# Softmax blocks transposed by DMA instead of TensorE in a two-layer decoder kernel

## Chip, cores and metric

The kernel runs on one core of a Trainium2 chip. The metric is the device time of one execution in microseconds (us).

## The reference, cut

One RG-LRU layer, then one layer of multi-head latent attention over shared keys and values. What matters here is the attention (1024 positions, 8 heads, blocks of 128 queries, all fp32):

```python
def one_block(args):                      # 128 queries of every head
    qn_b, qr_b, bi = args
    s = jnp.einsum("bqhd,bkhd->bhqk", qn_b, k_nope) + jnp.einsum("bqhr,bkr->bhqk", qr_b, k_rope)
    s = s * ATTN_SCALE
    mask = kpos[None, :] <= (bi * Q_BLOCK + jnp.arange(Q_BLOCK))[:, None]
    s = jnp.where(mask[None, None], s, -jnp.inf)
    p = jax.nn.softmax(s, axis=-1)
    return jnp.einsum("bhqk,bkhd->bqhd", p, v)
...
y = o.reshape(bsz, seq, N_HEADS * V_DIM) * jax.nn.silu(gate)
return y @ w_out                          # + residual, then a last rms_norm
```

## The kernel before

All products run on TensorE in a rounded fp32 format (`F32R`), three matmuls for one product: every operand is split by `hl` into a rounded part `hi` (on ACT) and a rest `lo` (on DVE), and hi*hi + hi*lo + lo*hi are summed in PSUM. The RG-LRU layer and the projections come first (about 530 us); their results wait in DRAM (`x1d`, `kvd`, `qsd`, the gates `gd`). SBUF holds most of its tiles in `NPAGES` = 36 pages of 128x1024 words.

The attention is a loop over 64 items (head `hd`, query block `qb`). In the order of the program:

- `scores` (lines 846 to 870): five matmuls per up to 512 keys into a PSUM tile `s` (two buffers, of two banks each), then on DVE the causal mask and the negative maximum, on ACT the exponential with its sum, on DVE the reciprocal and the scaling by it (line 869). The result `p_`, a page, has queries on the partitions and keys along the row. Scores are issued `LOOK` = 2 items ahead.
- `transposes` (872 to 881): the product with V needs keys on the partitions. TensorE transposes each 128x128 block against an identity into a PSUM bank `pm` (four buffers), up to four blocks to a bank; `hl` splits the bank into the `F32R` tiles `th`, `tl`. One item has qb+1 blocks.
- `pv` (883 to 902): per head twice, for query blocks 0 to 3 (g = 0) and 4 to 7 (g = 1), the product with V, three matmuls per block of keys, then the multiplication by the gate, and `hl` of the result `y`. The two halves of `y` of the first `NSPILL` = 6 heads go to DRAM (`ysd`, hi and lo, 512 KB each) and come back in `yload` near the end.

Between these stand pieces of other work that are due later, dealt out by lists with one entry for each `qb`: the next head's keys and queries (`KQ_AT`), values (`V0_AT`, `V_AT`), and in the last head the first pieces of the output product (`DPART`, `D_AT`, `dpart`), for which `wout` loads weights and `yload` loads `y`. A list `late` holds `pv` back by `PVD` = 1 items. The Tile framework writes the engines' queues from this program by a priority order and sets the semaphores; each engine works its queue in order.

Loads go through SP's queue; stores and the casting loads through GpSimd's (`DEPQ`).

After the loop the output product runs over three column chunks, with the last rms_norm at the end.

Of the kernel before, what the change touches and what calls it, by code (L numbers as in the profile page):

```python
# [10 lines left out]
F32R = mybir.dt.float32r  # L11
AF = mybir.ActivationFunctionType
# [26 lines left out]
D_AT = (0, 4, 1, 1, 1, 0, 3, 2)  # L39
PVD = 1  # L40
VQB = 4
# [16 lines left out]
def trunk(tc, xT, wina, vecs, wgate, wouta, winc, wuk, wuv, wuq, wuqr, woutb, rope, outT):  # L58
# [112 lines left out]
    pr_ = ExitStack()  # L171
    rbp = pr_.enter_context(tc.tile_pool(name="rbp", bufs=1))
# [83 lines left out]
    def xsplit(k, c=slice(0, S)):  # L256
        g = vec[:, NA + k:NA + k + 1]
        if len(xs) == k:
            xs.append((page(), page()))
# [199 lines left out]
    def fput(i, j, src):  # L459
        if fx[i][j // 2] is None:  # L460
            fx[i][j // 2] = (page(), page())
        hi, lo = fx[i][j // 2]
        hl(src, hi[:, hs(j % 2)], lo[:, hs(j % 2)])
# [382 lines left out]
    def scores(hd, qb, k, q, qs):  # L846
# [22 lines left out]
        V.tensor_scalar(out=p_[:, 0:nk], in0=p_[:, 0:nk], scalar1=l, scalar2=None, op0=ALU.mult)  # L869
        return p_  # L870

    def transposes(qb, p_, pts):
        for b0 in range(0, qb + 1, 4):
            b1 = min(qb + 1, b0 + 4)
            ps = pm()
            for b in range(b0, b1):
                T.transpose(out=ps[:, (b - b0) * P:(b - b0 + 1) * P], in_=p_[:, b * P:(b + 1) * P], identity=ident)  # L877
            th, tl = pts[b0 // 4]
            c = (qb % 4) * P
            src = ps[:, 0:(b1 - b0) * P].rearrange("p (k q) -> p k q", q=P)  # L880
            hl(src, th[:, 0:b1 - b0, c:c + P], tl[:, 0:b1 - b0, c:c + P])

    def pv(hd, g, pts):
# [3 lines left out]
        for b in range(nb):  # L887
            c = slice(max(0, b - 4 * g) * P, HW)
            vs = slice((b % 4) * 256 + (hd % 2) * P, (b % 4) * 256 + (hd % 2) * P + P)
            vh, vl = v[b // 4][0][:, vs], v[b // 4][1][:, vs]  # L890
            th, tl = pts[b // 4][0][:, b % 4, c], pts[b // 4][1][:, b % 4, c]
# [4 lines left out]
        V.tensor_tensor(out=y, in0=ps, in1=y, op=ALU.mult)  # L896
        if g == 0:
            ysb[hd] = (page(), page())
        hl(y, ysb[hd][0][:, hs(g)], ysb[hd][1][:, hs(g)])
        if hd < NSPILL and g == 1:  # L900
            for i in range(2):
                DQ.dma_start(out=ysd[hd, i], in_=f(ysb[hd][i]))
# [4 lines left out]
    ysd = dp.tile([NSPILL, 2, P, S], F32, name="ysd")  # L907
# [30 lines left out]
    kqwork = []  # L938
    vwork = vals(0, 0) + vals(0, 1)
    dwork = []  # L940
    ny = 0
    items = [(hd, qb) for hd in range(NH) for qb in range(8)]
    pend = {}
    pts = {}
    late = []
    for i in range(LOOK):
        pend[items[i]] = scores(*items[i], *heads[0])
    for i, (hd, qb) in enumerate(items):
        if qb == 0:
            gt = page(F32)  # L950
            nc.sync.dma_start(out=gt, in_=gd[hd])
            gates.append(gt)
            if hd + 1 < NH:
                heads[hd + 1], kqwork = kq(hd + 1)
        if qb == VQB and hd // 2 + 1 < NH // 2:
            vwork += vals(hd // 2 + 1, hd % 2)
        if i + LOOK < len(items):
            nh = items[i + LOOK]
            if nh[1] == 0 and nh[0]:
                while kqwork:  # L960
                    kqwork.pop(0)()
            pend[nh] = scores(*nh, *heads[nh[0]])
        if i == 8 * (NH - 1) + DSTART:
            dwork = [lambda a=a: dpart(*a) for a in DPART]
        for wl, n in ((kqwork, KQ_AT[qb]), (vwork, V0_AT[qb] if hd == 0 and qb < 4 else V_AT[qb]), (dwork, D_AT[qb - DSTART] if i >= 8 * (NH - 1) + DSTART else 0)):
            for _ in range(min(n, len(wl))):
                wl.pop(0)()
        g = qb // 4
        if qb % 4 == 0:
            pts[hd, g] = [tuple(tp.tile([P, 4, HW], F32R, tag=f"pt{i}", name=nm("pt")) for i in range(2)) for _ in range(g + 1)]  # L970
        if late and i - late[0][0] >= PVD:
            pv(*late.pop(0)[1:])
        transposes(qb, pend.pop((hd, qb)), pts[hd, g])
        if qb % 4 == 3:
            late.append((i, hd, g, pts.pop((hd, g))))
        j = i - 8 * (NH - 1)
# [137 lines left out]
```

## Time and profile before

| | |
|---|---|
| runs | 875.46 us median of 3 (875.23 to 875.82) |
| the profiled execution | 876.11 us; its span in the trace 874.3 us; granted TensorE clock 0.994 |
| busy, share of the span | TensorE 98%, weight load 83%, VectorE 75%, ScalarE 59%, GpSimd 9% |
| DMA | 109.00 MB, mean 125 GB/s |

The profile is one execution: it lists, for each engine (PE = TensorE matmul, PEld = its weight load, DVE = VectorE, ACT = ScalarE, POOL = GpSimd, SP = SyncE), the busy time, groups of like instructions by source line, and who waited for whom. Matmul durations overlap: one of 512 columns lasts about 0.39 us while the next starts after 0.23 us, so a group's busy time is more than what it adds to the span. A wait of an engine off the critical chain costs nothing.

### The profile page before, as it was taken

The numbers are of one execution on the slowest core, as the hardware profiler recorded it, in microseconds if no ns is written. First come the engines' busy times: TensorE is split into PE (matmuls) and PEld (weight loads), VectorE is DVE, ScalarE is ACT, GpSimd is POOL, SyncE is SP. The second block draws the span as 40 slices with busy tenths as digits, with TensorE's granted clock in tenths as the row PEclk, the third lists the DMA queues.
The fourth block names the chain that finished last, engine by engine and source line by source line (L and its number), as shares of the span: only waits on it lengthen the run. The fifth ranks groups of instructions, "written<-read, shape, count | busy, mean of one in ns | idle before, by whom it ended". The sixth has DMA issues, their size and how long they took to land.

```text
span 874.3 us, 12183 instructions
## 1 busy us (share of the span) xinstructions
PE 857.5 (98%) x4326; PEld 729.6 (83%) x4326; DVE 659.4 (75%) x1224; ACT 517.0 (59%) x956; POOL 75.1 (9%) x145
## 2 busy tenths in 40 slices
PE   8999999999999999999999999999999999999995
PEld 7788888888887888888778888988998998888995
DVE  7798778777877764779988956887797887775453
ACT  7457787777687542699885645555565554431222
POOL 1010110011000100000212320000000000010000
PEclk9999999999999999999999999999999999999998
DMA  8333333333212545133535664222231326666031
GB/s 289 99 97 97 97 96 97 109 101 92 79 37 81 179 132 175 49 108 111 177 122 205 216 229 119 76 82 97 70 112 67 111 67 258 214 216 204 27 126 66
DMA packets 51789, 109.00 MB, mean 125 GB/s; under 512 B 6544, under 2 KB 16656, under 8 KB 51728
## 3 DMA queue, kind: packets, MB, share of 16 engines
q1 hardware_dynamic: 36240, 67.45, 24.2%
q0 software_dynamic: 15216, 40.51, 13.9%
q8 instruction: 34, 0.56, 0.3%
q10 hardware_dynamic: 272, 0.26, 0.1%
q14 instruction: 27, 0.22, 0.1%
HBM read 81.46 MB, written 26.21 MB: 123 GB/s over the span
## 4 chain that ended last, share of the span: by engine, by line
PE 62%; issue 21%; DVE 7%; ACT 4%; DMA 2%; POOL 2%; SPq 0%; DVEq 0%; POOLq 0%; ACTq 0%
PE ps L115 7%; PE ps L116 7%; PE ps L114 7%; PE pm L116 6%; PE pm L115 6%; PE pm L114 6%; PE pm L877 4%; PE pm L894 2%; PE pm L893 2%; PE s L858 2%; PE s L859 2%; PE s L857 2%; PE s L861 2%; PE s L860 2%; PE pm L892 2%
## 5 line engine op out<-in xcount | busy, mean ns | idle before, releaser
L114 PE MATMUL ps<-pg,wh 128*128 128x512 f32 x672 | 262.4, 392 | 3.4 <-DVE tk L627 1.2
L115 PE MATMUL ps<-pg,wh 128*128 128x512 f32 x672 | 262.4, 390 | 0.3 <-DVE pg L262 0.3
L116 PE MATMUL ps<-pg,wl 128*128 128x512 f32 x672 | 262.2, 390 | 0.1
L114 PEld LDWEIGHTS ps<-pg,wh 128*128 128x128 f32 x672 | 126.4, 188 | 31.9 <-DVE tk L627 1.6
L115 PEld LDWEIGHTS ps<-pg,wh 128*128 128x128 f32 x672 | 126.5, 188 | 27.7 <-DVE pg L262 0.6
L116 PEld LDWEIGHTS ps<-pg,wl 128*128 128x128 f32 x672 | 126.6, 188 | 27.1 <-DVE wl L83 1.0
L82 ACT ACTIVATE pt<-pm 128x512 fp32r<-128x512 f32 (+2 forms) x96 | 44.4, 490 | 59.0 <-PE pm L877 55.8
L867 ACT ACTIVATE pg<-s,m 128x128 f32<-128x128 f32 (+3 forms) x64 | 47.5, 743 | 48.0 <-DVE m L864 43.3
L114 PE MATMUL pm<-pg,pg 128*128 128x256 f32 (+1 forms) x192 | 61.9, 322 | 0.0
L115 PE MATMUL pm<-pg,pg 128*128 128x256 f32 (+1 forms) x192 | 61.6, 321 | 0.0
L116 PE MATMUL pm<-pg,pg 128*128 128x256 f32 (+1 forms) x192 | 61.3, 319 | 0.0
L83 DVE TENSOR_TENSOR pt<-pm,pt 128x512 fp32r<-128x512 f32 (+2 forms) x96 | 50.6, 547 | 2.2 <-ACT pt L82 2.1
L864 DVE TENSOR_REDUCE m<-s 128x1 f32<-128x128 f32 (+3 forms) x64 | 48.1, 753 | 1.0
L83 DVE TENSOR_TENSOR wl<-wr,wh 128x512 fp32r<-128x512 f32 (+2 forms) x57 | 32.8, 578 | 17.2 <-ACT wh L82 17.1
L358 DVE SCALAR_TENSOR_TENSOR t<-xb,vec,t 128x512 f32<-128x512 f32 x60 | 44.8, 746 | 0.4
L82 ACT ACTIVATE wh<-wr 128x512 fp32r<-128x512 f32 (+2 forms) x57 | 30.8, 543 | 23.8 <-PE ps L115 9.7
L82 ACT ACTIVATE pg<-pg 128x512 fp32r<-128x512 f32 x42 | 26.2, 630 | 29.9 <-DVE pg L412 18.3
L877 PE MATMUL pm<-ident,pg 128*128 128x128 f32 x288 | 42.3, 274 | 0.3 <-DVE pg L869 0.3
L116 PE MATMUL pm<-pg,wl 128*128 128x512 f32 x108 | 42.3, 392 | 0.0
L115 PE MATMUL pm<-pg,wh 128*128 128x512 f32 x108 | 42.3, 392 | 0.0
L114 PE MATMUL pm<-pg,wh 128*128 128x512 f32 x108 | 42.1, 390 | 0.0
L857 PE MATMUL s<-pg,pg 128*128 128x512 f32 (+2 forms) x96 | 37.2, 388 | 2.0 <-ACT pg L867 2.0
(223 smaller groups left out, 1789.6 us busy)
## 6 DMA issues: line engine op xcount, KB each, us to landing
wr<-wina SPq DMA_DIRECT2D x40, 256.0 KB, 2.8
wh<-wina POOLq DMA_DIRECT2D x36, 256.0 KB, 2.9
wa<-winc SPq DMA_DIRECT2D x24, 256.0 KB, 2.7
ysd<-pg POOLq DMA_DIRECT2D x12, 512.0 KB, 3.2
pg<-ysd SPq DMA_DIRECT2D x12, 512.0 KB, 8.3
wr<-wouta SPq DMA_DIRECT2D x16, 256.0 KB, 2.7
t<-xT SPq DMA_DIRECT2D x16, 256.0 KB, 4.0
x1d<-t POOLq DMA_DIRECT2D x16, 256.0 KB, 3.4
```

Source lines behind the costliest of these rows:

```text
L82: A.activation(out=hi, in_=src, func=AF.Copy)
L83: V.tensor_tensor(out=lo, in0=src, in1=f(hi), op=ALU.subtract)
L114: T.matmul(out=ps, lhsT=w[0], rhs=r[0], start=first, stop=False, skip_group_check=more)
L115: T.matmul(out=ps, lhsT=w[0], rhs=r[1], start=False, stop=False, skip_group_check=more)
L116: T.matmul(out=ps, lhsT=w[1], rhs=r[0], start=False, stop=last, skip_group_check=more)
L358: V.scalar_tensor_tensor(out=xc, in0=xb[:, j:j + HW], scalar=cwv[j], in1=xc, op0=ALU.mult, op1=ALU.add)
L857: T.matmul(out=sc[:, c], lhsT=q[0][:, ql], rhs=k[0][:, c], start=True, stop=False)
L858: T.matmul(out=sc[:, c], lhsT=q[0][:, ql], rhs=k[1][:, c], start=False, stop=False)
L859: T.matmul(out=sc[:, c], lhsT=q[1][:, ql], rhs=k[0][:, c], start=False, stop=False)
L864: V.tensor_reduce(out=m, in_=sc, axis=AX.X, op=ALU.max, negate=True)
L867: A.activation(out=p_[:, 0:nk], in_=sc, func=AF.Exp, bias=m, accum_out=l)
L877: T.transpose(out=ps[:, (b - b0) * P:(b - b0 + 1) * P], in_=p_[:, b * P:(b + 1) * P], identity=ident)
```

## The change

The softmax block is transposed on its way through DRAM. DMA's transpose moves 2-byte words; so GpSimd copies the fp32 block, seen as pairs of half words, into two planes (all low halves, then all high halves), stores them to a DRAM tile `z`, and SP loads `z`, seen as 256 rows (query, half) of nk words, transposed: what lands in SBUF has a key on each partition and, along the row, the two halves of each query's word side by side, that is the fp32 block transposed. `psplit` then splits it by `hl` into one pair of tiles for each (head, g), from SBUF and no longer from PSUM, one call per item. It runs `HLAG` = 3 items after the item's scores. The normalisation moves from DVE to ACT. `scores` are no longer issued ahead of their item, and the lists that deal out the other work are new.

For the first six heads `y` is stored as it is (fp32, 512 KB a head, in two halves) instead of split; `yload` loads it once through SP and once, with a cast to `F32R`, through GpSimd, and DVE subtracts. `NPAGES` falls to 32; `NX` = 4 pages of their own hold the first input tiles (`xsplit`, `fput`) until the attention, whose tiles then take their place. The early part of the output product covers three column tiles (`DPART`) instead of two.

```diff
-NPAGES = 36
+NPAGES = 32
+NX = 4
 NSPILL = 6
-WOUT_AT = (-1, 1, 2)
-YL_AT = (0, 0, 0, 0, 1, 2)
-DSTART = 0
-DPART = tuple((dt, k, k + 1) for dt in range(2) for k in range(6))
+WOUT_AT = (-2, -1, 1)
+YL_AT = (-1, 0, 0, 0, 1, 3)
+DSTART = 1
+DPART = tuple((dt, k, k + 1) for k in range(6) for dt in range(3))
-LOOK = 2
-KQ_AT = (1, 0, 1, 0, 2, 0, 0, 0)
-V0_AT = (1, 1, 2, 0)
-V_AT = (0, 0, 0, 0, 0, 0, 1, 1)
-D_AT = (0, 4, 1, 1, 1, 0, 3, 2)
-PVD = 1
-VQB = 4
+KQ_AT = (1, 1, 1, 0, 1, 0, 0, 0)
+V_AT = (0, 0, 0, 0, 1, 1, 1, 1)
+VQB = 3
+GQB = 5
+D_AT = (2, 2, 2, 2, 2, 1, 1)
+HLAG = 3
+PVL = 1
+ROW = 384
...
         V.reciprocal(out=l, in_=l)
-        V.tensor_scalar(out=p_[:, 0:nk], in0=p_[:, 0:nk], scalar1=l, scalar2=None, op0=ALU.mult)
-        return p_
-
-    def transposes(qb, p_, pts):
-        for b0 in range(0, qb + 1, 4):
...
-                T.transpose(out=ps[:, (b - b0) * P:(b - b0 + 1) * P], in_=p_[:, b * P:(b + 1) * P], identity=ident)
...
-            hl(src, th[:, 0:b1 - b0, c:c + P], tl[:, 0:b1 - b0, c:c + P])
+        A.activation(out=p_[:, 0:nk], in_=p_[:, 0:nk], func=AF.Copy, scale=l)
+        c = pgs.tile([P, 2 * S], U16, tag="pg", name=nm("pu"))
+        G.tensor_copy(out=c[:, 0:2 * nk].rearrange("p (t n) -> p t n", t=2),
+                      in_=p_.bitcast(U16)[:, 0:2 * nk].rearrange("p (n t) -> p t n", t=2))
+        z = dp.tile([P, 2 * nk], U16, name=nm("z"))
+        G.dma_start(out=z, in_=c[:, 0:2 * nk])
+        nc.sync.dma_start_transpose(out=c[:, 0:2 * nk].rearrange("p (b q) -> p b q", q=2 * P), in_=z.rearrange("q (t n) -> (q t) n", t=2))
+        return c
+
+    def psplit(qb, c, pt):
+        src = c.bitcast(F32)[:, 0:(qb + 1) * P].rearrange("p (b q) -> p b q", q=P)
...
+        hl(src, block(pt[0]), block(pt[1]))
...
         V.tensor_tensor(out=y, in0=ps, in1=y, op=ALU.mult)
-        if g == 0:
-            ysb[hd] = (page(), page())
-        hl(y, ysb[hd][0][:, hs(g)], ysb[hd][1][:, hs(g)])
-        if hd < NSPILL and g == 1:
-            for i in range(2):
-                DQ.dma_start(out=ysd[hd, i], in_=f(ysb[hd][i]))
+        if hd < NSPILL:
+            DQ.dma_start(out=ysd[hd, :, hs(g)], in_=y)
+        else:
+            if g == 0:
+                ysb[hd] = (page(), page())
+            hl(y, ysb[hd][0][:, hs(g)], ysb[hd][1][:, hs(g)])
...
     def yload(hd):
-        ysb[hd] = (page(), page())
-        for i in range(2):
-            nc.sync.dma_start(out=f(ysb[hd][i]), in_=ysd[hd, i])
+        hi, lo = ysb[hd] = (page(), page())
+        nc.sync.dma_start(out=f(lo), in_=ysd[hd])
+        G.dma_start(out=hi, in_=ysd[hd])
+        V.tensor_tensor(out=lo, in0=f(lo), in1=f(hi), op=ALU.subtract)
...
     for i, (hd, qb) in enumerate(items):
+        g = qb // 4
+        j = i - 8 * (NH - 1)
         if qb == 0:
+            while kqwork:
+                kqwork.pop(0)()
+        cs_[i] = scores(hd, qb, *heads[hd])
+        if qb == 0 and hd + 1 < NH:
+            heads[hd + 1], kqwork = kq(hd + 1)
+        if qb == VQB and hd % 2 == 0:
+            vwork = vals(hd // 2, 0)
+        elif qb == VQB + 2 and hd % 2 == 0:
+            vwork += vals(hd // 2, 1)
+        if qb == GQB:
             gt = page(F32)
             nc.sync.dma_start(out=gt, in_=gd[hd])
             gates.append(gt)
...
+        if i >= HLAG:
+            hd_, qb_ = items[i - HLAG]
+            if qb_ % 4 == 0:
+                n = 8 * HW if qb_ else 4 * ROW + P
+                pts[hd_, qb_ // 4] = tuple(tp.tile([P, n], F32R, tag=f"pt{qb_}{a}", bufs=1, name=nm("pt")) for a in range(2))
+            psplit(qb_, cs_.pop(i - HLAG), pts[hd_, qb_ // 4])
+            if qb_ % 4 == 3:
+                late.append((i, hd_, qb_ // 4, pts.pop((hd_, qb_ // 4))))
+        if late and i - late[0][0] >= PVL:
             pv(*late.pop(0)[1:])
-        transposes(qb, pend.pop((hd, qb)), pts[hd, g])
...
+    for i in range(len(items) - HLAG, len(items)):
+        hd, qb = items[i]
+        psplit(qb, cs_.pop(i), pts[hd, qb // 4])
+    while dwork:
+        dwork.pop(0)()
+    late.append((0, NH - 1, 1, pts.pop((NH - 1, 1))))
     while late:
         pv(*late.pop(0)[1:])
-    while dwork:
-        dwork.pop(0)()
```

More of the change, by code (lines that the diff above doesn't have):

```diff
@@ L11 @@
 F32R = mybir.dt.float32r
+U16 = mybir.dt.uint16
 AF = mybir.ActivationFunctionType
@@ L258, in xsplit @@
         if len(xs) == k:
-            xs.append((page(), page()))
+            xs.append((page(), page()) if k >= NX // 2 else (xpage(), xpage()))
         xh, xl = xs[k][0][:, c], xs[k][1][:, c]
@@ L952, in trunk @@
             gates.append(gt)
[L953 to L963, printed above, removed]
+        if j == DSTART:
             dwork = [lambda a=a: dpart(*a) for a in DPART]
-        for wl, n in ((kqwork, KQ_AT[qb]), (vwork, V0_AT[qb] if hd == 0 and qb < 4 else V_AT[qb]), (dwork, D_AT[qb - DSTART] if i >= 8 * (NH - 1) + DSTART else 0)):
+        for wl, n in ((kqwork, KQ_AT[qb]), (vwork, V_AT[qb]), (dwork, D_AT[j - DSTART] if j >= DSTART else 0)):
             for _ in range(min(n, len(wl))):
                 wl.pop(0)()
[L968 to L971, printed above, removed]
+        if i >= HLAG:
[7 more added lines that the diff above has]
+        if late and i - late[0][0] >= PVL:
             pv(*late.pop(0)[1:])
-        transposes(qb, pend.pop((hd, qb)), pts[hd, g])
-        if qb % 4 == 3:
-            late.append((i, hd, g, pts.pop((hd, g))))
-        j = i - 8 * (NH - 1)
         for _ in range(YL_AT.count(j)):
```

37 lines of the change are left out of this document (19 added, 18 removed).

## The prediction

> **What bounds the kernel now.** I read the page's heads first, then the stage in which the transposes stand, then the PE timeline inside it, and last the waits. The page:
>
> ```profile
> span 874.3 us, 12183 instructions
> PE 857.5 (98%) x4326; PEld 729.6 (83%) x4326; DVE 659.4 (75%) x1224; ACT 517.0 (59%) x956; POOL 75.1 (9%) x145
> PE   8999999999999999999999999999999999999995
> ```
>
> TensorE (PE) is busy from end to end; GpSimd (POOL) has nearly nothing to do. The transposes (line 877) all lie in the stretch from 534 to 778 us. Busy time by stretches (columns: PE, weight load, DVE, ACT, POOL, clock, DMA share, GB/s), the group of the transposes, and the waits of this stretch:
>
> ```profile
> 534.00:778.00 244.00, 242.79 (x1449) 216.73 (x1450) 201.27 (x447) 131.72 (x299) 10.17 (x20) 1.00 0.35 117
> 650.00:680.00 30.00, 30.00 (x180) 26.92 (x180) 24.77 (x56) 17.23 (x39) 1.06 (x2) 1.00 0.27 89
> 740.00:770.00 30.00, 28.79 (x165) 24.81 (x164) 24.53 (x56) 13.84 (x33) 1.06 (x2) 1.00 0.60 213
> 770.00:800.00 30.00, 30.00 (x147) 24.97 (x146) 19.78 (x34) 7.20 (x13) 2.65 (x5) 1.00 0.81 267
> ...
> L877 PE MATMUL pm<-ident,pg 128*128 128x128 f32 x288 | 42.3, 274 | 0.3 <-DVE pg L869 0.3
> ...
> ACT pt L82 <- PE pm L877: 55.8, 39, 3.4
> PE s L857 <- ACT pg L867: 2.0, 2, 1.1
> ```
>
> In 244 us PE stands still for about 1 us. The other engines wait for PE (ACT for transposes, 55.8 us); PE waits for nobody (2.0 us in all). Eight heads share the stretch: 30.5 us each, at the full granted clock (1.00). So whatever leaves PE shortens the stage, as long as nobody else becomes late.
>
> **What leaves PE.** 288 transposes (8 heads, 36 blocks of 128x128 each). The 42.3 us of the group overlap with the next matmul, so I take start-to-start times from PE's timeline (columns: start, duration):
>
> ```profile
> 649.04 0.39 PE L861 MATMUL s<-pg,qs 128*128 128x512 f32 x1
> 649.27 0.81 PE L877 MATMUL pm<-ident,pg 128*128 128x128 f32 x6
> 649.84 0.31 PE L857 MATMUL s<-pg,pg 128*128 128x128 f32 x1
> ...
> 663.15 0.30 PE L877 MATMUL pm<-ident,pg 128*128 128x128 f32 x1
> 663.21 0.48 PE L857 MATMUL s<-pg,pg 128*128 128x512 f32 x1
> ...
> 776.61 1.03 PE L877 MATMUL pm<-ident,pg 128*128 128x128 f32 x8
> 777.40 0.48 PE L115 MATMUL pm<-pg,pg 128*128 128x512 f32 x1
> 777.72 0.40 PE L116 MATMUL pm<-pg,pg 128*128 128x512 f32 x1
> 777.95 0.39 PE L114 MATMUL pm<-pg,pg 128*128 128x512 f32 x1
> ```
>
> Six take 0.57 us until the next matmul starts, eight 0.79, one 0.06: about 0.096 each, 27.6 us for 288. The matmul behind a group takes 0.32 (777.40 to 777.72) where one of its size takes 0.23: 0.085 more, 64 groups, 5.4 us. **33 us** leave PE, 4.1 per head; 26.4 per head remain.
>
> **What takes their place.** For each of the 64 items (a head, a query block qb with nk = 128(qb+1) keys): the normalisation moves from DVE to ACT; GpSimd copies 2nk half words into two planes and issues a store to DRAM; SP waits for that store and issues the transposing load; ACT and DVE split what comes back (`psplit`), three items later (HLAG = 3). The rows nearest to these steps (line, out<-in, shape, count; busy, mean ns):
>
> ```profile
> L862 DVE TENSOR_TENSOR s<-s,mask 128x128 f32<-128x128 f32 x62 | 18.3, 295 | 9.8 <-PE s L861 9.1
> L864 DVE TENSOR_REDUCE m<-s 128x1 f32<-128x1024 f32 x8 | 9.8, 1224 | 0.3
> L867 ACT ACTIVATE pg<-s,m 128x1024 f32<-128x1024 f32 x8 | 8.9, 1117 | 2.0 <-DVE m L864 2.0
> L867 ACT ACTIVATE pg<-s,m 128x512 f32<-128x512 f32 x8 | 5.5, 690 | 5.5 <-DVE m L864 5.5
> L867 ACT ACTIVATION_READ_ACCUMULATOR pg<-s,m 128x1 f32 x63 | 12.2, 194 | 0.0
> L868 DVE RECIPROCAL l<-l 128x1 f32<-128x1 f32 x64 | 10.2, 159 | 14.4 <-ACT pg L867 13.4
> L82 ACT ACTIVATE pg<-pg 128x512 fp32r<-128x512 f32 x15 | 9.5, 631 | 3.6 <-DVE pg L896 3.2
> L869 DVE TENSOR_SCALAR pg<-pg,l 128x128 f32<-128x128 f32 (+3 forms) x64 | 33.1, 517 | 1.4
> ...
> L902 POOL DMA_DIRECT2D ysd<-pg x12 | 6.4, 534 | 198.6 <-ACT pg L82 194.1 <-DVE pg L869 2.9 <-DVE pg L83 1.5
> L1058 POOL TENSOR_TENSOR pg<-pg,acc 128x256 f32<-128x256 f32 x2 | 1.8, 898 | 88.9 <-DVE acc L151 88.9
> L168 POOL TENSOR_SCALAR_AFFINE_SELECT mask<-mask 128x128 f32<-128x128 f32 x1 | 0.3, 286 | 0.0
> L167 POOL MEMSET mask<- 128x128 f32 x1 | 0.2, 204 | 0.0
> L1106 POOL MEMSET const-float32-0.0<- 128x1 f32 x1 | 0.1, 98 | 0.2 <-issue 0.2
> ...
> ysd<-pg POOLq DMA_DIRECT2D x12, 512.0 KB, 3.2
> gd<-tk POOLq DMA_DIRECT2D x16, 256.0 KB, 2.9
> pg<-gd SPq DMA_DIRECT2D x8, 512.0 KB, 4.0
> wr<-wuv SPq DMA_DIRECT2D x8, 256.0 KB, 2.7
> pg<-pg POOLq DMA_DIRECT2D x4, 128.0 KB, 5.4
> ```
>
> *Engine loads.* ACT has 132 us of work in this stretch; the normalisation adds about 64 items at the mean length of an exponential, some 42, so 174 of 211. DVE loses the 33.1 of line 869 and has 168. Both fit, so I cost them at nothing as loads; as steps of the chain below they count.
>
> *GpSimd's copy.* No row shows it. Low end, MEMSET: (204 - 98)/127 = 0.83 ns an element. High end, the two-input TENSOR_TENSOR: (898 - 98)/255 = 3.1 ns. I take AFFINE_SELECT, the only row with one input and one output: (286 - 98)/127 = 1.5 ns. For qb = 7, 2048 half words: 3.2 us (1.8 to 6.5); for qb = 3, 1.6 (0.9 to 3.3). All 288 blocks of 256 half words: 110 us (61 to 229), and 64 issues of 0.53, 34 us. At 1.5 ns GpSimd is busy 144 of 211 us.
>
> *The transposing load.* No row either. Low end: a plain load of as many bytes, 4.0 us for 512 KB (`pg<-gd`), 2.7 for 256 KB. High end: the slowest transfer per byte that rearranges partitions, `pg<-pg`, 128 KB in 5.4 us, so 21 us for 512 KB. I take 1 to 1.3 times the plain load, since it is a load of whole rows from DRAM like `pg<-gd`; the high row is a transfer of 32 partitions at a time.
>
> The Trainium skill, "DMA: Bandwidth & Descriptors", Latency and other measured facts, gives 261 GB/s for a DMA transpose whose rows do not lie together; as an estimate from that page 512 KB move in 2.0 us beside a plain load's fixed part, which would leave the sum where the plain rows put it. No run here shows it.
>
> *The chain against the lag.* ACT and DVE work in order. `psplit` of item i stands in ACT's queue behind the exponential of item i+3, so the exponential of i+4 starts after the split of i (if the program's order is the engines' order). Eight items of one head are thus two loops behind each other: the chain of qb = 7 and then that of qb = 3 must fit into one head's period. From the start of the exponential to the end of the split's copy:
> qb = 7: 1.12 + 0.19 + 0.16 + 1.12 (scale) + 3.2 (copy) + 3.2 (store) + 4.0 (load) + 1.1 (split) + 1.0 for seven hand-overs = 15.1 us.
> qb = 3: 0.69 + 0.19 + 0.16 + 0.69 + 1.6 + 2.9 + 2.7 + 0.63 + 1.0 = 10.6 us.
> Together 25.7 us, 6.7 of them the transposing loads. PE needs 26.4 per head. With plain-speed loads the chain hides, with 0.7 us to spare; at 1.3 times it takes 27.7 and PE waits 1.3 us per head, 10 us in all. I take the middle: **+5 us**.
>
> *The tail.* Before, the last block's transposes sit on PE with products as filler, and PE is 30.00 of 30 us busy in 770 to 800. After, behind the last scores come mask 0.30, maximum 1.22, the chain of 15.1 and the split's subtraction, together about 18 us, before the last product with V can end its sums. PE has `pv` of the first half (12 matmuls, 3840 columns at 0.23 us for 512, 1.7 us) and the 6 pieces of `DPART` that `D_AT` leaves over (18 - 12; 3 matmuls of 0.23 us each, 4.1 us). **+12 us** idle.
>
> *SP's and GpSimd's queues.* The transposing load waits on SP for its store; behind it stand the weights' loads, `qs`, the gates, `wout` and `yload`. They are wanted one or more items later, 3.3 us each on average, so I cost this at nothing; without that cover it is up to the chain's store time, 3 us per head, 24 us. On GpSimd the `y` stores and the loads of `hi` in `yload` and `wout` stand behind copies of up to 3.2 us; the same cover.
>
> *y as fp32.* Six spilled heads store 512 KB instead of 1 MB and lose their split on ACT and DVE; `yload` gains one subtraction of 128x1024 per head on DVE. PE does not see it: nothing. The pages set aside for `xs` (NX) change no order in which PE works: nothing, and a page wait of a few us if that cover fails.
>
> *DMA.* Per head 36 blocks of 64 KB go out and come back, 2.36 MB each way. The row of 650 to 680 us moves 89 GB/s at a share of 0.27, so about 330 GB/s would fill the engines: 14.3 us more beside 8.1 - 1.6 (half of y's store), 20.8 of 26.4. It fits in heads 0 to 5. At 740 to 800 us the share is already 0.60 to 0.81.
>
> **Sum**, against the profiled execution's own 876.1 us (span 874.3 and 1.8 around it; the median of the runs is 875.5): 876.1 - 33 + 12 + 5 = **860 us**.
>
> **The rivals.**
> 1. *The chain outruns the lag* (the other side). Speaks for it: 0.7 us of cover per head, two prices that no row shows. Against: it needs the load at more than 1.48 times a plain one: (244 - 12)/8 = 29 us per head is the point of no change. At twice, 32.4 us per head: 8 x 32.4 + 12 = 271 against 244, 903 us. The GpSimd copy at the high row adds 5.0 per head alone: 30.7, 258, 890 us.
> 2. *DMA binds in the last two heads.* For: 0.60 x 30 + 14.3 = 32 us and 0.81 x 30 + 14.3 = 39 us of transfers in periods of 26.4, so up to 18 us of queue. Against: part of those loads (`wout`) is wanted only later. All of it on the path: 878 us; most likely half, 869 to 875.
> 3. *All hidden*, the tail too, because instructions are reordered: 876.1 - 33 = 843 us. Against: after the last scores PE has 6 us of work left by the loop's own lists.
> 4. *Half-word blocks pass one behind another.* If the high row `pg<-pg` holds for the load, the chains take 19 + 21 + 11 = 51 us per head: 8 x 51 + 12 = 420, 1052 us. For it: the only row that crosses partitions is also the slowest per byte. Against: that row has 32 partitions per transfer.
>
> The Trainium skill, "VectorE: DVE Perf Modes", The three transpose paths, speaks against the change: it gives 1309 ns for a 128x128 block of 2-byte words by DMA against 390 ns on TensorE, and advises TensorE where the result may go to PSUM. Taken as a rate, 576 such blocks are an estimated 754 us, far beyond the stage; taken as one transfer's latency it changes nothing, and no row here tells which. The trace's TensorE transposes last 274 ns (the group's mean), below that page's figure.
>
> **How the numbers follow.** Forecast (848 to 868) 0.48; all hidden (840 to 848) 0.09; DMA in the last heads (868 to 878) 0.11; chain outruns the lag (878 to about 930) 0.26; rival 4 (over 1000) 0.06. The time is that of the first, 860. The range 842 to 908 leaves out rival 4, half of rival 1 and a little of rival 3, 2 in 10. Within 0.2% (1.8 us) a measurement of this kernel cannot tell a change from none. Faster: 0.48 + 0.09 + half of 0.11, 0.62. Same: 0.04. Slower: 0.02 + 0.26 + 0.06 = 0.34.
>
> **What would show it.** Right: line 877 gone and PE near 100% from about 540 to 740 us, a stage some 16 us shorter, one PE gap of about 12 us before the last `pv`, GpSimd busy some 140 us, landings of the transposing loads near 3 to 5 us. Rival 1: ACT waiting in `psplit` for a DMA in every head, PE waiting in line 857 for ACT. Rival 2: DMA share at 1.0 only in the last two heads, and gaps there. The prediction falls if the transposing load lands in over 6 us at 512 KB or GpSimd's copy takes over 2 ns an element: then the chain, not PE, is the period.

## The result and the profile after

The changed kernel takes 967.83 us (median of 4; 965.33 to 969.71) against 875.4: a ratio of 1.105 (95% interval 1.103 to 1.108), 92 us slower, outside the range of 842 to 908. The page of the profiled execution, in the rows shown of before:

```profile
span 965.3 us, 11979 instructions
PE 861.1 (89%) x4038; PEld 716.6 (74%) x4038; DVE 640.1 (66%) x1122; ACT 553.1 (57%) x976; POOL 190.0 (20%) x279
PE   8999999999999999999999869889878845849994
DMA packets 131662, 143.61 MB, mean 149 GB/s; under 512 B 83344, under 2 KB 93456, under 8 KB 131600
```

PE was 98% busy and is 89% busy; its holes lie in the attention. The transposes are gone, yet PE's busy time grew by 4 us; that matmuls last longer where the granted clock drops is likely, and was not tested by itself. The windows say where (columns as before: five engines, clock, DMA share, GB/s), and the waits of the stretch from 520 to 890 us say for whom:

```profile
535.00:858.00 323.00, 247.91 (x1186) 205.67 (x1184) 180.47 (x344) 166.79 (x319) 123.80 (x151) 0.88 0.72 190
650.00:680.00 30.00, 24.79 (x119) 20.76 (x119) 17.63 (x35) 16.41 (x33) 12.50 (x15) 0.94 0.65 184
780.00:820.00 40.00, 16.16 (x53) 11.76 (x52) 17.79 (x28) 8.56 (x17) 10.76 (x16) 0.62 0.89 264
```

```profile
POOL pu L882 <- ACT pg L878: 164.4, 50, 12.2
ACT pt L85 <- DMA pu<-z: 96.6, 41, 9.1
DVE pt L86 <- ACT pt L85: 72.2, 36, 4.1
PEld s L866 <- ACT pg L876: 48.2, 23, 9.7
PE s L866 <- ACT pg L876: 40.7, 19, 9.6
```

Before, PE waited 2.0 us in the stage and the others waited for PE. Now no engine is full in 650 to 680 us (PE 24.79 of 30, DVE 17.63, ACT 16.41, GpSimd 12.50), and one circle of waits holds all: ACT's split (line 85) waits for the transposing load, 96.6 us; behind it in ACT's queue stand exponentials (line 876); the scores (line 866) wait for the exponential to free their PSUM buffer. These are the two waits that the prediction named for its first rival.

The first exponential of each head, read off ACT's timeline, gives the period of each head. The same reading for the main experiments (us; the last column runs from the last exponential to the span's end):

| kernel | first head | heads 1 to 5, sum | head 6 | head 7, to its last exponential | behind |
|---|---|---|---|---|---|
| before | 26.3 | 155.0 | 31.3 | 27.4 | 100.9 |
| after | 31.0 | 181.8 | 46.5 | 53.1 | 117.9 |
| e1, before without transposes | 24.4 | 138.2 | 28.0 | 27.4 | 98.5 |
| e2, after, late output work | 29.9 | 182.9 | 40.2 | 27.6 | 143.1 |
| e5, after without the trip | 25.2 | 143.2 | 35.0 | 44.6 | 100.4 |
| e8, e2 with a held lag of 3 | 31.8 | 168.8 | 39.7 | 26.0 | 145.6 |
| e9, e2 with a held lag of 4 | 24.3 | 162.7 | 33.6 | 29.4 | 146.6 |
| e10, e9 with plain loads | 24.3 | 148.0 | 31.0 | 27.0 | 140.6 |
| e11, before, part of the blocks by DMA in heads 0 to 6 | 29.7 | 151.9 | 30.7 | 37.1 | 101.3 |
| e14, the same in heads 1 to 5 | 26.3 | 152.7 | 31.6 | 27.4 | 100.7 |

So the 91 us between the spans of before and after are 1.6 ahead of the stage, 4.7 in head 0, 26.8 in heads 1 to 5, 40.9 in the last two, 17.0 behind.

Why ACT waits so much with a lag of three items is seen in its own timeline, here head 2 (start, duration, ACT's instruction, idle before). The width names the item: an exponential (L876) of 640 is qb = 4, a split `pt<-pu` of 640 is the split of that same item.

```profile
601.47 0.35 ACT L876 ACTIVATE pg<-s,m 128x128 f32<-128x128 f32 x1
...
612.16 0.68 ACT L876 ACTIVATE pg<-s,m 128x512 f32<-128x512 f32 x1
...
614.05 1.06 ACT L85 ACTIVATE pt<-pu 128x1024 fp32r<-128x1024 f32 x1 [1.12 <-DMA pu<-z]
615.63 0.29 ACT L85 ACTIVATE pt<-pu 128x128 fp32r<-128x128 f32 x1
615.83 0.77 ACT L876 ACTIVATE pg<-s,m 128x640 f32<-128x640 f32 x1
616.60 0.40 ACT L85 ACTIVATE pt<-pu 128x256 fp32r<-128x256 f32 x1
620.18 0.53 ACT L85 ACTIVATE pt<-pu 128x384 fp32r<-128x384 f32 x1 [1.78 <-DMA pu<-z]
623.96 0.63 ACT L85 ACTIVATE pt<-pu 128x512 fp32r<-128x512 f32 x1 [1.49 <-DMA pu<-z]
626.45 0.74 ACT L85 ACTIVATE pt<-pu 128x640 fp32r<-128x640 f32 x1 [1.37 <-DMA pu<-z]
627.57 0.90 ACT L876 ACTIVATE pg<-s,m 128x768 f32<-128x768 f32 x1
...
633.63 1.12 ACT L876 ACTIVATE pg<-s,m 128x1024 f32<-128x1024 f32 x1
...
637.01 0.37 ACT L876 ACTIVATE pg<-s,m 128x128 f32<-128x128 f32 x1 [0.71 <-DVE m L873]
...
649.32 1.04 ACT L85 ACTIVATE pt<-pu 128x1024 fp32r<-128x1024 f32 x1
```

The program puts the split of item i behind the exponential of i+3. Here the split of qb = 4 stands ahead of the exponential of qb = 5: four splits of blocks stand in a row, 616.60 to 627, three of them waiting for their load, and the lag falls from three to none. The order of an engine's queue is written by the framework's scheduler, not by the program's text. Heads 1, 2, 4 and 6 have such a row of splits, heads 3 and 5 have pairs, and from qb = 5 of head 6 to qb = 2 of head 7 one exponential and one split alternate: a lag of one.

The lengths themselves. GpSimd's longest copy (form, count, then busy and mean ns):

```profile
L882 POOL COPY pu<-pg 128x2048 uint16<-128x2048 uint16 x8 | 15.2, 1898 | 10.9 <-ACT pg L878 10.9
```

The stores and the transposing loads (KB each, where it is given, and median us from issue to landing):

```profile
z<-pu POOLq DMA_DIRECT2D x8, 512.0 KB, 5.1
z<-pu POOLq DMA_DIRECT2D x8, 256.0 KB, 2.7
z<-pu POOLq DMA_DIRECT2D x8, 64.0 KB, 4.7
pu<-z SPq DMA_TRANSPOSE x64, 3.9
```

In head 2 the chain of qb = 7 runs from 633.63 to the end of ACT's split at 650.36: 16.7 us where 15.1 were estimated; that of qb = 3 from 612.16 to 624.59: 12.4 where 10.6 were. Together 29.1, not 25.7 (30.7 as the mean of heads 1 to 5).

### The profile page after: what moved, and what is told of

Its sections match the earlier page's. It is cut to its first block, busy times and chain, and to the rows that moved or that the text cites. A ratio compares the mean times of both kernels' runs of the same rounds, so it can differ in the third digit from the quotient of the medians.

```text
span 965.3 us, 11979 instructions
## 1 busy us (share of the span) xinstructions
PE 861.1 (89%) x4038; PEld 716.6 (74%) x4038; DVE 640.1 (66%) x1122; ACT 553.1 (57%) x976; POOL 190.0 (20%) x279
## 3 DMA queue, kind: packets, MB, share of 16 engines
q1 hardware_dynamic: 111152, 83.18, 31.2%
## 4 chain that ended last, share of the span: by engine, by line
issue 33%; PE 28%; DMA 13%; POOL 10%; DVE 8%; ACT 7%; SPq 0%; POOLq 0%; DVEq 0%; ACTq 0%
DMA pu<-z 6%; PE ps L118 6%; PE ps L117 6%; PE ps L119 6%; POOL pu L882 4%; PE pm L117 3%; PE pm L118 3%; PE pm L119 3%; POOL z L885 2%; DMA z<-pu 2%; DMA pg<-woutb 1%; DVE t L367 1%; ACT pt L85 1%; DVE t L418 1%; DVE wl L86 1%
## 5 line engine op out<-in xcount | busy, mean ns | idle before, releaser
L117 PE MATMUL ps<-pg,wh 128*128 128x512 f32 x568 | 220.7, 390 | 2.5 <-DVE tk L636 1.3
L118 PE MATMUL ps<-pg,wh 128*128 128x512 f32 x568 | 221.1, 389 | 0.1
L119 PE MATMUL ps<-pg,wl 128*128 128x512 f32 x568 | 220.9, 389 | 0.2 <-DVE wl L86 0.2
L117 PEld LDWEIGHTS ps<-pg,wh 128*128 128x128 f32 x568 | 106.4, 188 | 25.9 <-DVE tk L636 1.7
L118 PEld LDWEIGHTS ps<-pg,wh 128*128 128x128 f32 x568 | 106.6, 188 | 22.7 <-DVE pg L86 0.5
L882 POOL COPY pu<-pg 128x256 uint16<-128x256 uint16 (+3 forms) x64 | 77.5, 1214 | 170.5 <-ACT pg L878 164.4
L86 DVE TENSOR_TENSOR pt<-pu,pt 128x128 fp32r<-128x128 f32 (+3 forms) x64 | 53.9, 850 | 74.9 <-ACT pt L85 72.2
L85 ACT ACTIVATE pt<-pu 128x128 fp32r<-128x128 f32 (+3 forms) x64 | 43.6, 681 | 96.7 <-DMA pu<-z 96.6
L878 ACT ACTIVATE pg<-pg,l 128x128 f32<-128x128 f32 (+3 forms) x64 | 49.5, 774 | 36.2 <-DVE l L877 36.1
L915 PE MATMUL pm<-pt,pg 128*128 128x512 f32 (+1 forms) x96 | 36.4, 379 | 23.9 <-ACT pt L85 23.9
L866 PEld LDWEIGHTS s<-pg,pg 128*128 128x128 f32 x96 | 20.3, 211 | 50.4 <-ACT pg L876 48.2
L876 ACT ACTIVATE pg<-s,m 128x128 f32<-128x128 f32 (+3 forms) x64 | 47.0, 735 | 18.1 <-DVE m L873 11.5
L117 PEld LDWEIGHTS pm<-pg,pg 128*128 128x128 f32 x192 | 37.0, 193 | 21.7 <-DMA pg<-ysd 7.7
L85 ACT ACTIVATE wh<-wr 128x512 fp32r<-128x512 f32 (+2 forms) x57 | 30.5, 539 | 31.2 <-PE pm L118 14.6
```

The costliest lines, as they stand in the source:

```text
L85: A.activation(out=hi, in_=src, func=AF.Copy)
L86: V.tensor_tensor(out=lo, in0=src, in1=f(hi), op=ALU.subtract)
L117: T.matmul(out=ps, lhsT=w[0], rhs=r[0], start=first, stop=False, skip_group_check=more)
L118: T.matmul(out=ps, lhsT=w[0], rhs=r[1], start=False, stop=False, skip_group_check=more)
L119: T.matmul(out=ps, lhsT=w[1], rhs=r[0], start=False, stop=last, skip_group_check=more)
L866: T.matmul(out=sc[:, c], lhsT=q[0][:, ql], rhs=k[0][:, c], start=True, stop=False)
```

## The experiments

**e1: the transposes' worth by themselves.** The kernel before without its 288 transposes; nothing is transposed.

```diff
-            ps = pm()
-            for b in range(b0, b1):
-                T.transpose(out=ps[:, ...], in_=p_[:, b * P:(b + 1) * P], identity=ident)
-            src = ps[:, 0:(b1 - b0) * P].rearrange("p (k q) -> p k q", q=P)
+            src = p_[:, b0 * P:b1 * P].rearrange("p (k q) -> p k q", q=P)
```

> The kernel before, with the transposes left out: the split reads the untransposed block from SBUF, 288 TensorE transposes are gone and nothing takes their place (the product with V then sums the wrong elements). It measures the term 'what leaves PE' by itself. By the prediction 33 us: 876 - 33 = 843, PE still busy all through. If TensorE's real share of the transposes were only their weight loads or less, 855 to 865; if it were the whole 42 us of the group, 833.

852.44 us, 0.974 (0.971 to 0.977): 23 us, 0.08 us a transpose, not 33. The middle window and the waits of the stage show what takes PE's place:

```profile
650.00:680.00 30.00, 29.45 (x165) 26.08 (x164) 27.02 (x61) 17.66 (x40) 1.11 (x3) 1.00 0.26 90
```

```profile
ACT pg L867 <- DVE m L864: 54.7, 38, 4.2
PE s L857 <- ACT pg L867: 6.8, 8, 3.4
```

PE is no longer at 30.00 of 30, and DVE is at 27.02: the maximum (line 864) comes late, ACT waits for it 54.7 us (40.0 in the same stage before), and PE waits for ACT's exponential 6.8 us (2.0 before). That is part of the missing 10 us. Over the whole span PE's busy time falls by 29.4 us (857.5 to 828.1) and its idle time grows by 5.7 (16.8 to 22.5), so some 4 us were priced too high on PE itself and some 6 went into waits. This DVE still does the scaling (line 869), which the change gives to ACT; how much of the 6 that would return was not measured.

**e2: the output's early work taken out of the loop.** The changed kernel with its weights, `y` loads and pieces left to the end.

```diff
-WOUT_AT = (-2, -1, 1)
-YL_AT = (-1, 0, 0, 0, 1, 3)
-DPART = tuple((dt, k, k + 1) for k in range(6) for dt in range(3))
+WOUT_AT = ()
+YL_AT = ()
+DPART = ()
```

> The changed kernel with the output product's early work (three weight tiles, the loads of y, 18 early pieces) put behind the attention loop: WOUT_AT, YL_AT and DPART empty. Theory A (the last two heads are slow because those loads and pages crowd the transposing chain): heads 6 and 7 fall from 46.6 and over 60 us to the 35.5 of heads 1 to 5, 35 us gained, of which the product and its loads, no longer hidden, give back 15 to 25: 945 to 955. Theory B (the chain with its transfers is slow wherever it stands): heads 6 and 7 stay slow, 975 to 990.

960.43 us, 1.097 (1.094 to 1.100). The last two heads fall from 99.6 to 67.8 us, but what stands behind the loop grows by 25. So this early work does cost the last heads 32 us, and most of it is only moved: theory A for the heads, but 960 where it wanted 955 at most. The middle heads stay (182.9).

**e3 and e4: the queues in the program's order.** e3 is e2 with ACT and DVE told to keep the program's order in the loop; e4 has plain loads beside that.

```diff
+    ms = ExitStack()
+    ms.enter_context(tc.manual_schedule(engines={_E.Activation, _E.DVE}))
     for i, (hd, qb) in enumerate(items):
```

> As e2_late, and ACT and DVE work through the attention loop in the order of the program instead of the framework's: every split stands three items behind its exponential, where in the changed kernel four splits in a row stand ahead of the exponential of qb = 5 in heads 1, 2, 4 and 6. Theory order (these early splits make ACT wait for a load that was just issued): the head period falls from 35.5 to the two measured chains, about 17 + 12.5 = 29.5 us, 6 us a head: 35 to 45 us less than e2_late, 900 to 915. Theory transfers (the chain is slower than the lag in any order): within 10 us of e2_late.

> As e3, with a plain load of the same bytes in place of the transposing load, and GpSimd's copy without setting the halves apart (the block is then not transposed, which leaves out the transposing). It measures the crossbar's part. If the transposing load is about as quick as a plain one (the prediction): within 8 us of e3. If it is the slow step (1.33 us of SP's queue each and 256-byte pieces): its two loads per head shorten by 2 us or more each, and the period falls by 4 us to PE's 26.4, 25 to 30 us less than e3.

1052.5 us, 1.202 (1.199 to 1.206), and 1043.21, 1.192 (1.187 to 1.196). The waits of e3 from 560 to 900 us:

```profile
ACT pg L876 <- DVE m L873: 129.3, 49, 5.2
PEld s L866 <- ACT pg L876: 95.2, 39, 5.9
```

In the written order the maximum comes late on DVE, ACT waits for it 129.3 us, and the loads hardly matter (9 us between the two, near the 8 of e4's first forecast). Neither theory foresaw this, and the pair cannot tell whether the lost lag is the cause. It shows that the program's order, which the prediction took for the engines', is slower still when ACT and DVE both keep it.

**e5: the trip taken away.** The split reads GpSimd's copy; nothing goes to DRAM, the blocks are not transposed. The copy is plain here (no setting apart) and as long as before: 1.90 us for qb = 7 in both.

```diff
...
-        z = dp.tile([P, 2 * nk], U16, name=nm("z"))
-        G.dma_start(out=z, in_=c[:, 0:2 * nk])
-        nc.sync.dma_start_transpose(out=..., in_=z.rearrange("q (t n) -> (q t) n", t=2))
```

> The changed kernel without the way through DRAM: GpSimd copies the block (without setting the halves apart, the same number of elements) and the split reads that copy, so nothing is transposed. Loop, lists, pages, y, the scaling on ACT and GpSimd's copies stay. Theory round trip (store, wait and transposing load are what the stage waits for): the head periods fall from 35.5 to the 27.7 of the kernel before without transposes, and the last two heads with them: 850 to 870. Theory loop (scores no longer issued ahead, the scaling on ACT, GpSimd's copy and the new lists cost by themselves): periods stay above 31, 900 or more.

885.01 us, 1.010 (1.008 to 1.012): the trip, with what the scheduler orders otherwise because of it, is worth 83 of the 92 us; scaling on ACT, GpSimd's copy and the new lists are not what costs these 83. But the kernel is still 33 us above e1: 5 in heads 1 to 5, 24 in the last two. There (735 to 790 us) the waits are

```profile
ACT pg L878 <- DVE l L877: 20.4, 6, 9.4
PE pm L117 <- DMA pg<-ysd: 16.3, 2, 8.6
```

PE stands at an early output piece until its `y` has come. These loads go out late: the first at 734.2 us, 3.7 us before the head's first exponential, where the kernel before issues it at 730.2, 15.8 us before.

**e6: plain loads in the changed kernel.** GpSimd's copy is plain too, again of the same length.

```diff
...
-        nc.sync.dma_start_transpose(out=..., in_=z.rearrange("q (t n) -> (q t) n", t=2))
+        nc.sync.dma_start(out=c[:, 0:2 * nk], in_=z)
```

> The changed kernel with a plain load in place of the transposing one (no setting apart, nothing transposed); the store to DRAM stays. If the crossbar's load is the slow step (its 256-byte pieces also fill the DMA engines): 30 us or more gained, 935 or less, DMA share in the stage down by a third. If any way through DRAM is too long for the order in which ACT works: within 15 us of 967.8.

953.43 us, 1.088 (1.085 to 1.091). The transposing itself is 14 of the 92 us, inside the 15 of the second forecast; a trip of plain transfers in this order is nearly as bad.

**e7: `y` as fp32, alone, in the kernel before.**

```diff
-            for i in range(2):
-                DQ.dma_start(out=ysd[hd, i], in_=f(ysb[hd][i]))
+            DQ.dma_start(out=ysd[hd, :, hs(g)], in_=y)
...
-            nc.sync.dma_start(out=f(ysb[hd][i]), in_=ysd[hd, i])
+        nc.sync.dma_start(out=f(lo), in_=ysd[hd])
+        G.dma_start(out=hi, in_=ysd[hd])
+        V.tensor_tensor(out=lo, in0=f(lo), in1=f(hi), op=ALU.subtract)
```

> The kernel before with the y edit alone (one fp32 store per half head, yload with a casting load and a subtraction). Prediction: nothing, 875.4 within 1.8 us. If the six subtractions and casting loads, late in the last head, come onto the path: up to 880.

879.87 us, 1.004 (1.003 to 1.006): 4 us, and nothing but head 7 is longer (32.1 instead of 27.4), where the weight loads of PE's early pieces wait for the new subtraction (line 913), in a row that the kernel before does not have:

```profile
PEld pm L115 <- DVE pg L913: 4.1, 4, 1.9
```

**e8 and e9: the lag kept by hand.** e2 with each split held behind the exponential and the reciprocal that are three (e8) or four (e9, `HLAG = 4`) items later; ACT's order is otherwise the scheduler's. `last` holds the newest exponential and reciprocal.

```diff
+            with tc.issue_after(last['a'].ins), tc.issue_after(last['v'].ins):
                 psplit(qb_, cs_.pop(i - HLAG), pts[hd_, qb_ // 4])
```

> As e2_late (960.4), and each split is held behind the exponential (ACT) and the reciprocal (DVE) of the item three later; everything else keeps the framework's order, so ACT and DVE are not put in lockstep as in e3. Theory order (the framework puts splits early, in a row, because its model lands their loads sooner than the chip does): the head period of 35.6 falls to about the two chains, 29.5 to 31, 920 to 930. Theory round trip at any place (bandwidth, or the queues of SP and GpSimd): period 34 to 36, 950 to 965.

> As e8 with the splits four items behind (HLAG = 4). Theory order, and chain against lag: one more item covers 3.5 us more of each chain, so the period falls to the 27.7 to 29 of the kernel without a round trip, 900 to 912. If e8 already lies at 28, nothing more. Theory round trip: as e8 within 5 us.

948.66 us, 1.084 (1.078 to 1.090), and 933.14, 1.066 (1.063 to 1.069): 12 and 27 us below e2. ACT's timeline shows the lag kept at three or more, and at four, until the end of the last head. The order alone, at lag three, is worth 12 us where theory order wanted 30 to 40; one more item is worth 15 more, and 933 misses the 900 to 912 of that theory as well as the 5 us of the other. A middle head takes 33.8 us in e8 and 32.5 in e9 instead of 36.6, in e9 still 1.6 above the kernel before. Its window:

```profile
650.00:680.00 30.00, 25.47 (x138) 21.52 (x137) 18.33 (x39) 17.59 (x35) 14.69 (x18) 1.00 0.94 218
```

The clock is granted in full again, PE has 4.5 us of idle time, and the DMA share is 0.94.

**e10: e9 with plain loads.** The edit is e6's, on e9.

> The kernel of e9 (splits four blocks later, held; no work of the output's first pages inside the loop) with a plain load in place of the transposing one and a plain copy on GpSimd; the blocks are not transposed, the bytes are the same. Theory A, with the lag held the DMA engines' time is what is left: in e9 their share was 0.85 to 0.94 in the middle heads, and the transposing loads take about 33 us more of it than plain ones (18.9 MB at about 210 against 330 GB/s). Then the middle heads go from 32.6 us to 28.5 to 30, and 933 to 905 to 915 us. Theory B, what is left is the length of one trip and the order of the instructions: the middle heads stay at 31.5 or more, and the time is 925 to 933 us.

908.21 us, 1.037 (1.035 to 1.039), 25 us below e9; a middle head takes 29.6 us. The same stretch:

```profile
650.00:680.00 30.00, 28.48 (x165) 25.07 (x164) 22.26 (x42) 20.09 (x40) 14.60 (x18) 1.00 0.69 220
```

As many bytes per second (220 against 218) take a share of 0.69 instead of 0.94. So with the lag held, the DMA engines' time is what binds in e9: theory A. The edit also shortens the issue of a load on SP, from 1.8 us in the mean to 0.33, and does not separate the two. But the long issues are themselves seen with full engines: in e9 ten took more than 2 us, at a DMA share of 1.00 while they lasted, and 35 took less than 1.4, at 0.58. In e6, where the lag was lost, the same edit gave 14. This kernel's loop, 230 us from the first exponential of head 0 to the last of head 7, is 10 us shorter than the kernel before's, 240; it loses 40 behind the loop, where the output's early work stands since e2.

**e11 and e12: part of the blocks.** The kernel before, `y` and all, with some query blocks of the first seven heads by DMA and GpSimd and the rest on TensorE: blocks 0, 1, 4, 5 in e11 (14 of 36 blocks of 128x128 a head), also 2 and 6 in e12 (24 of 36). Their splits are held until the exponentials of qb = 3 and 7.

```diff
+VIA = {0: 3, 1: 3, 4: 7, 5: 7}
...
-        transposes(qb, pend.pop((hd, qb)), pts[hd, g])
+        if qb in VIA and hd in range(NH - 1):
+            pass
+        else:
+            transposes(qb, pend.pop((hd, qb)), pts[hd, g])
+        for b in [b for b in VIA if VIA[b] == qb and hd in range(NH - 1)]:
+            with tc.issue_after(last['a'].ins), tc.issue_after(last['v'].ins):
+                psplit(b, pend.pop((hd, b)), pts[hd, g])
```

> The kernel before with 14 of the 36 blocks of a head (query blocks 0, 1, 4 and 5) in the first seven heads taken through DRAM and the transposing load; their splits are held until the exponentials of query blocks 3 and 7, two or more blocks later; the other blocks and the whole last head stay on TensorE, y stays as it was. Theory A, a trip costs nothing if the lag covers it and the DMA engines have room: 98 of the 288 transposes of a block leave TensorE at 23 us / 288 = 0.08 us each (from e1), so 875.4 - 7.8 = 868 us, a ratio of 0.991, and heads of 29.7 us instead of 31.0. Theory B, the waits come back in small: heads of 31 us or more, 875 us or above.

> As e11, with 24 of the 36 blocks of a head (query blocks 0, 1, 2, 4, 5 and 6) taken through DRAM in the first seven heads; the split of blocks 2 and 6 follows one block behind. Theory A: 168 transposes leave TensorE, 875.4 - 13.4 = 862 us, a ratio of 0.985. Theory B, the blocks that have one block's time for their trip (exponential to split about 10 to 17 us in the changed kernel, a block's period about 4 us) stop ACT in its queue by 6 us or more, twice a head: heads of 33 us or more, 890 us or above.

887.73 us, 1.014 (1.012 to 1.015), and 893.05, 1.020 (1.018 to 1.021): theory A falls for both. But the reason is not what theory B says. In e11 a middle head takes 30.4 us, 0.6 less than before. The loss is 3.4 us in head 0 and 9.7 in head 7, which has no block by DMA. At 750 to 770 us PE is 15.1 of 20 us busy at a DMA share of 0.66 to 1.01, and the chain of waits there holds one piece of 8.49 us for `y`:

```profile
757.57 8.49 DMA pg<-ysd
```

The loads of `y` are the same as before, but they go out some 24 us later: SP, which issues them, first waits for the stores of head 6's blocks, 22.6 us between 715 and 765 us. SP's queue in e11 (two rows, then the wait), and the same loads in e14, where heads 0 and 6 have no trips:

```profile
727.55 17.28 SPq L881 DMA_TRANSPOSE pu<-z  x3
753.74 7.03 SPq L932 DMA_DIRECT2D pg<-ysd  x10
SPq L881 <- DMA z<-pu: 22.6, 4, 8.4
```

```profile
728.92 11.70 SPq L932 DMA_DIRECT2D pg<-ysd  x10
```

In e12 a middle head takes 30.8 us where theory B wanted 33; its total lies where theory B put it, for this other reason.

**e13: the early output pieces taken away.** The changed kernel with `DPART = ()` alone; weights and `y` are loaded as early as before.

> The changed kernel without the early pieces of the output projection in the last head (its weight and y loads stay early, ACT's order of exponentials and splits stays the same within one split). Theory A, the last head is long because these pieces stop TensorE's queue until their y block is loaded, behind which the scores stand: its 53.1 us fall to 36 to 42; the work of the pieces comes back behind the loop, 8 to 14 us. Theory B, it is long because the trips of the blocks are slower there, beside the loads: it stays at 48 us or more, and the whole is 5 to 12 us slower than the changed kernel.

981.13 us, 1.121 (1.116 to 1.125). Theory A falls: the last head stays at 53.0 us. PE's waits from 745 us on, of the changed kernel and of e13:

```profile
PE s L866 <- ACT pg L876: 14.1, 4, 9.6
PE pm L117 <- DMA pg<-ysd: 13.7, 2, 7.2
```

```profile
PE s L866 <- ACT pg L876: 30.6, 8, 8.6
PE pm L915 <- ACT pt L85: 28.3, 2, 19.3
```

The wait for `y` goes and the wait for exponentials grows by about as much: PE would have stood there anyway. The pieces were filler, and without them the waits before `pv` (line 915) grow by 13 us, as much as the whole loss.

**e14: the middle heads alone.** e11 with the trip in heads 1 to 5.

```diff
...
-        if qb in VIA and hd in range(NH - 1):
+        if qb in VIA and hd in range(1, NH - 2):
...
```

> As e11, with the trip through DRAM in heads 1 to 5 alone; the first head and the last two as before the change. In e11 a middle head took 30.4 us against 31.0, the first 3.4 us more and the last 9.7 us more than before. Theory A, these losses belong to the heads beside the stage's other transfers: they go, and five heads keep 0.5 to 0.6 us each, 872.5 to 873.5 us, a ratio of 0.997. Theory B, the trips push other work (the y stores and loads) behind the stage: 876 us or more.

873.65 us, 0.997 (0.996 to 0.998): theory A, and the last head is back at 27.4 us. A version faster than both kernels, by 0.3%, that is 2.3 us over five heads, 14 blocks of each off TensorE.

```profile
650.00:680.00 30.00, 29.18 (x171) 25.82 (x170) 26.00 (x57) 16.66 (x39) 8.53 (x10) 1.00 0.55 152
```

70 transposes at e1's 0.08 us would give 5.6; PE is idle 0.8 of 30 us, with DVE at 26.00.

## Why the prediction was wrong

*The step that failed* is "The chain against the lag" and its +5 us: the trip through DRAM was to hide behind the lag of three items, and it costs 83 (e5). Three parts of that step were wrong: the order, the chain's length, and the DMA time that was held to fit beside it. Taken away one on top of the other, they are 12, 15 and 25 us of the 85 of e2; none alone explains the loss.

*The order.* The step assumed the split of i behind the exponential of i+3, "if the program's order is the engines' order". It is not. The scheduler writes splits ahead of exponentials, in heads 1, 2, 4 and 6 the lag falls to none, and every load that has not landed stops ACT, and through the exponentials PE. e8 undoes this alone: 12 us of e2's 85.

*The chain was short by 3.4 us in head 2.* 29.1 against 25.7, more than PE's 26.4 of work. GpSimd's copy was priced too high: 2048 half words took 1.90 us (0.93 ns each; 1.5 was assumed, the low end 0.83). Both transfers were priced too low. The store of 512 KB takes 5.1 us (3.2 came from `ysd<-pg`). The load's median of 3.9 us is over all sizes; in the trace the eight loads of qb = 7 land after 4.2 to 5.7 us, median 5.1, those of qb = 3 after 3.3 to 5.4, median 3.8: 8.9 together where 6.7 was priced, the 1.3 times that the prediction had as its upper end. In head 2 the store and the load of qb = 7 take some 10 us of its 16.7. A lag of four instead of three gave 15 us more (e8 to e9).

*DMA's time was computed at one rate for all.* The fit into heads 0 to 5 used 330 GB/s. Queue 1's share of the span, over 16 engines, shows otherwise:

```profile
q1 hardware_dynamic: 36240, 67.45, 24.2%
```

```profile
q1 hardware_dynamic: 111152, 83.18, 31.2%
```

```profile
q1 hardware_dynamic: 44592, 83.18, 27.7%
```

In turn before, after and e6. 31.2% of 965.3 is 301 us, before 212: 89 us for 15.7 MB more (18.9 of `z`, less 3.1 of `y`), where plain loads of the same bytes in e6 make it 264, that is 52; at 330 GB/s it would be 48. Queue 1 grew by 75,000 packets with the transposing load and by 8,400 with the plain one: 18.9 MB in that many packets are some 250 bytes each. This is worth 25 us once the lag is held (e9 to e10) and 14 where it is not (e6). The Trainium skill, "VectorE: DVE Perf Modes", The three transpose paths, gives 1309 ns for a 128x128 block of 2-byte words by DMA. The 576 blocks added 89 us of all 16 engines, about 0.15 us a block: as a rate that page's figure would have made an estimated 754 us, so here it is no rate. The Trainium skill's advice on the same page (Rules for kernel authors), TensorE where the result may go to PSUM, agrees with this result: the way over TensorE is the faster one here.

*The 33 us were 23* (e1). PE's busy time fell by 29 of the 33, so the term itself was some 4 too large. The other 6 are waits: DVE was busy 24.77 of 30 us beside PE, and with PE relieved its maximum is late. By e1 "all hidden" was worth 852, not 843.

*`y` as fp32 was costed at nothing* and is 4 us (e7): it puts a load, a casting load and a subtraction in front of the early pieces, in the last head.

*SP's queue was costed at nothing*, with "they are wanted one or more items later" as the cover. That cover fails: in e11 the `y` loads stand 22.6 us behind transposing loads that wait for their stores, and the last head is 9.7 us longer; without trips in heads 0 and 6 both go (e14). In the changed kernel SP waits for such stores 71.5 us between 690 and 850 us; what that costs there was not taken apart.

*The last two heads.* Rival 2 named them and priced them at 18 us at most; they lost 41. Of that 21 stay without any trip (e5 against before), and 32 go with the output's early work (e2). The early pieces do not cause it (e13). One thing goes with the long head in every trace: in the changed kernel, e6 and e13 ACT alternates one exponential and one split from qb = 5 of head 6 on, a lag of one, and the last head takes 51 to 53 us, with plain loads too; in e2 the same splits stand two to five exponentials behind, and it takes 27.6. But whether it is this order, the pages that the output's loads hold or the DMA share (0.89 in 780 to 820 us, 0.71 in e2) is not separated: e2 changes all three.

*The rivals.* The first came true by its two signs, ACT waiting in `psplit` and PE at the scores, but its price (890 to 903) hung on a load at twice a plain one or a slow copy. The load was 1.3 times, the copy quick. It was given 0.26 and a point of no change at 29 us a head; the head became 36.4.

*What was right.* Line 877 gone; the gap before the last `pv`: 12 us predicted, and the wait in that place has 11.6 as its longest:

```profile
PE pm L915 <- ACT pt L85: 15.1, 2, 11.6
```

The size agrees in part by luck: the prediction had 18 us less 6 of other work for PE; in the trace 21.6 us lie between the last scores and this product, and PE has 10 of other work. GpSimd is no bound, though its busy time in the stage is 124 and not 140. The sign of falling that the prediction named, over 2 ns an element or a 512 KB landing over 6 us, did not appear. It fell without them, on the order, on the sum of several small prices and on the DMA time; the order had no sign of its own there.

An account, as far as it goes: of 92 us, the trip is 83 (e5). From e2, holding the lag at three, then at four, then plain loads take 12, 15 and 25 away. The 33 that e10 is above the kernel before are 40 behind the loop and some 2 ahead of it, against 10 won in it. Of the stretch behind the loop, 25 us came with the output's early work put there (e2 against the changed kernel), and 17 the changed kernel has already.

## What to carry to other kernels

A software lag in the source is a wish as long as a scheduler writes the queues: read the engine's own timeline and count how many items stand between an operation and its late consumer, before a latency is called hidden. Price a trip through DRAM by the landing of both its transfers, look at what stands behind their waits in the issuing queue, and check that the DMA engines have the time at the rate of *that* transfer's packets. And where an engine is 98% busy, look at who is next (here DVE at 0.8 of PE) before all its saved time is counted: take it away once, as e1 did, and see.

## What the runs showed of the hardware

- A transposing load occupies SP's queue 1.33 us (up to 3.59) for its issue (the row has minimum, median and maximum in ns), where the plain loads next to it take 0.37 and 0.58:

```profile
L886 SPq DMA_TRANSPOSE pu<-z x64: 1130/1332/3594, 538.7 to 859.7; - x64
```

```profile
641.60 0.58 SPq L822 DMA_DIRECT2D qs<-qsd  x1
642.27 0.37 SPq L94 DMA_DIRECT2D wr<-wuv  x1
643.82 4.14 SPq L886 DMA_TRANSPOSE pu<-z  x2
```

- At the same 220 GB/s the DMA share is 0.94 with transposing loads and 0.69 without (e9, e10).
- A store of 64 KB landed after 4.7 us in the median, later than one of 256 KB (2.7). It is issued in GpSimd's queue right behind the 512 KB store of the item before; in head 0, where none stands ahead, it landed after 1.8 us. That it waits behind the larger one is likely, and not tested.
- The granted clock is 0.62 in the stretch of the changed kernel where PE is 16 of 40 us busy (780 to 820 us), and 1.00 in e9 with PE busy 25.5 of 30 (650 to 680 us): long stalls of PE and a lower clock were seen together.
